# Low parts of weights made by an accumulating DMA in every fourth group of a two-layer decoder trunk

## The chip, the cores and the metric

The kernel runs on one core of one Trainium2 chip. The metric is the time of one execution in device microseconds; of several runs the median is taken. A core has five engines that matter here: TensorE (PE in the profile, its weight loads PEld), VectorE (DVE), ScalarE (ACT), GpSimd (POOL) and SyncE (SP). Each takes its instructions in order and waits on semaphores of the others.

## The reference

Two layers work on x of 256 rows and 2048 columns, all in float32. Cut to its products, a layer is:

```python
h = rmsnorm(x, norm_mix_g[i]);  proj = h @ w_in[i]      # 2048 x 9224
y_conv = conformer_conv(glu_in, ...)                    # depthwise conv, width 31, layernorm, silu, @ w_conv_out
y_attn = forgetting_attention(q, k, v, log_f) @ w_attn_out[i]      # 8 heads of 128
x = x + (sigmoid(g_conv) * y_conv + sigmoid(g_attn) * y_attn) @ w_out[i]
gate, up = split(rmsnorm(x, norm_ffn_g[i]) @ w_gate_up[i])         # 2048 x 11264
x = x + (silu(gate) * up) @ w_down[i]                              # 5632 x 2048
x = x + sigmoid(rmsnorm(x, norm_ple_g[i]) @ w_ple_gate[i]) * (p[i] @ w_ple_proj[i])
```

and a last rmsnorm follows. All weights together are some 540 MB, and each is used once.

## The kernel before, in words

Every large product runs through `chunk`: 512 columns of the output for all 256 rows, in two PSUM banks (`mm`), over groups of four blocks of 128 rows of the weight. A group is one `load`: one DMA on SP's queue brings 128 x 2048 float32 (1 MB) into a `raw` buffer, of which there are three. Then the group is split into two tiles of 1024 columns, and each tile into two parts of type float32r: the high part `wh` is the weight rounded to float32r by ScalarE (L147), and the low part `wl` is the raw weight less the high part, by VectorE (L148). The activations are split in the same manner. For each block of the weight and each half of the rows, three matmuls follow (L168 to L170): high by high, high by low part of the weight, low by high. A tile has twelve such matmuls, a group twenty-four. Of `wh` and of `wl` there are four buffers each, so a tile is prepared while up to three others are consumed, and a `raw` buffer is free for the next load when both of its tiles are converted.

There are 512 groups: 144 for `w_in` (`wI`), 16 each for `w_attn_out` and `w_conv_out` (`wA`, `wC`), 32 for `w_out`, 176 for `w_gate_up` (`wGU`), 88 for `w_down` (`wD`), 32 for `w_ple_gate` (`wPG`), and 8 of half the width for `w_ple_proj` (`wPP`). The very first group is loaded in pieces (`hook`).

Beside the products run the depthwise convolution (L336, VectorE), the attention (L495 to L532), the norms and the transposes that turn results into operands. `conv_norm` scales the convolution's result (L590 to L594) and splits it (L186, L187). Where these stand among the weights' conversions is decided by a scheduler, which orders each engine's instructions when the program is built; on each engine they then run in that order. POOL has little to do: memsets and the reciprocal square roots of the norms (L239, `rt`, and L260, `small`).

Of the kernel before, what the change touches and what calls it, by code (L numbers as in the profile page):

```python
# [12 lines left out]
AF = mybir.ActivationFunctionType  # L13
ALU = mybir.AluOpType
# [29 lines left out]
def trunk(ctx, tc, xT, xR, pT, wI, wF, wC, wA, wOut, wGU, wD, wPG, wPP, vec, bF, gF, out):  # L44
    nc = tc.nc
# [11 lines left out]
    act, dve, pe = nc.scalar, nc.vector, nc.tensor  # L57
# [70 lines left out]
    nc.gpsimd.memset(lf, 0.0)  # L128


    def load(src, n=2048, hook=None):
        raw = raws.tile([P, 2048], F32, tag="raw", name=f"raw{next(uid)}")
        if hook is None:
            nc.sync.dma_start(raw[:, :n], src)
        else:
            nc.sync.dma_start(raw[:, :512], src[:, :512])
            nc.sync.dma_start(raw[:, 512:1024], src[:, 512:1024])
            hook()
            nc.sync.dma_start(raw[:, 1024:], src[:, 1024:])
        parts = []  # L140
        step = 1024 if hook is None else 512
        for lo in range(0, n, 1024):
            h = whs.tile([P, 1024], F32R, tag="wh", name=f"wh{next(uid)}")
            l = wls.tile([P, 1024], F32R, tag="wl", name=f"wl{next(uid)}")
            for o in range(0, 1024, step):
                e = o + step
                act.activation(h[:, o:e], raw[:, lo + o : lo + e], AF.Copy)  # L147
                dve.tensor_tensor(l[:, o:e], raw[:, lo + o : lo + e], h[:, o:e].bitcast(F32), op=ALU.subtract)  # L148
            parts.append((h, l))
        return parts  # L150
# [3 lines left out]
    def chunk(groups, xs, acc, hook=None):  # L154
        n = sum(len(ks) for _, ks in groups)
        done = 0
        for src, ks in groups:
            parts = load(src, 512 * len(ks), hook)
            hook = None
            while not all(k in xs for k in ks):  # L160
                assert turns or tasks
                run()
            for j, k in enumerate(ks):
                h, l = parts[j // 2]
                cs = slice((j % 2) * 512, (j % 2 + 1) * 512)
                for b in range(2):
                    xh, xl = xs[k][:, b * P : (b + 1) * P], xs[k][:, S + b * P : S + (b + 1) * P]
                    pe.matmul(acc[b], lhsT=xh, rhs=h[:, cs], start=(done == 0), stop=False)  # L168
                    pe.matmul(acc[b], lhsT=xh, rhs=l[:, cs], start=False, stop=False)  # L169
                    pe.matmul(acc[b], lhsT=xl, rhs=h[:, cs], start=False, stop=(done == n - 1))  # L170
                done += 1
            run()
            fill(CONV)
        return acc
# [117 lines left out]
    def hook():  # L292
        load_x(0, 2, 4)
        take(0)
# [17 lines left out]
    for i in range(L):  # L312
# [392 lines left out]
        def embed(n):  # L705
            return chunk([(wPP[i, n], range(2))], ps, [bank_ms() for _ in range(2)])
# [6 lines left out]
        for n in range(N4):  # L713
            e = embed(n)
# [85 lines left out]
```

## Time and profile before

| | |
|---|---|
| median of 3 runs | 2903.79 us (2902.66 to 2904.2) |
| the profiled execution | 2902.9 us |
| its span in the profile | 2900.8 us |
| TensorE's granted clock | 0.998 |
| read from HBM | 538.91 MB, 187 GB/s over the span |

The profile is one execution seen by the hardware profiler, with times in us from the start of the span. A row of a timeline gives the start, the duration, the engine, the line of the kernel, the operation, what it writes and reads, how many instructions are merged in the row, and in brackets for how long the engine had been idle and what ended the idle time. A row of a group gives total busy time and the mean in ns of one, then the idle time ahead of the group. A row of waits gives who waited for whom, the total in us, how often, and the longest. Matmuls overlap, so the spacing of their starts tells more than their durations.

### The profile page before, as it was taken

What the parts mean: (1) busy time and instruction counts of PE and PEld (TensorE: products, weight loads), DVE (VectorE), ACT (ScalarE), POOL (GpSimd) and SP (SyncE); (2) the same over time, 40 slices, a digit from 0 to 9 for tenths busy, and PEclk for the clock granted to TensorE, in tenths of its full rate; (3) what the DMA queues carried; (4) which work ended last, traced back from release to release, by engine and by line L of the source; (5) the groups of instructions that cost most, each with busy time, mean ns of one, the idle gap of its engine ahead of it and who ended that gap; (6) DMA issues with size and microseconds to landing.
All of it is one profiled execution on the core that took longest, in us unless ns stands there. A gap on an engine that the chain in (4) does not pass through costs nothing.

```text
span 2900.8 us, 32675 instructions
## 1 busy us (share of the span) xinstructions
PE 2876.6 (99%) x13004; PEld 2381.2 (82%) x13004; DVE 1751.8 (60%) x2264; ACT 1356.2 (47%) x1642; POOL 9.5 (0%) x40
## 2 busy tenths in 40 slices
PE   8999999999999999999999999999999999999998
PEld 6888888888888888888888888888888888888886
DVE  5997745555555555555569966465555555455554
ACT  5445744444444434445554456444443444344444
POOL 0000000000000000000000000000000000000000
PEclk9999999999999999999999999999999999999999
DMA  7554455555555555555555544555555555555553
GB/s 271 174 186 163 170 193 189 189 185 188 193 188 189 192 193 193 189 188 183 186 181 181 183 166 174 190 188 189 188 189 188 190 191 189 198 190 188 189 195 139
DMA packets 77048, 543.11 MB, mean 187 GB/s; under 512 B 8800, under 2 KB 9056, under 8 KB 12256
## 3 DMA queue, kind: packets, MB, share of 16 engines
q1 hardware_dynamic: 76896, 541.04, 53.2%
q8 instruction: 101, 1.65, 0.2%
q14 instruction: 51, 0.42, 0.0%
HBM read 538.91 MB, written 2.10 MB: 187 GB/s over the span
## 4 chain that ended last, share of the span: by engine, by line
PE 94%; DVE 4%; DMA 1%; ACT 0%; issue 0%; SPq 0%; POOL 0%; ACTq 0%; POOLq 0%; DVEq 0%
PE mm L170 30%; PE mm L168 30%; PE mm L169 30%; PE ms L199 2%; DVE pair L336 2%; DVE wl L148 2%; DMA xt<-in_xR_dram 1%; PE ms L495 0%; PE ms L170 0%; PE ms L169 0%; PE ms L168 0%; PE ms L531 0%; DMA pair<-in_xT_dram 0%; ACT tmp L221 0%; PE ms L497 0%
## 5 line engine op out<-in xcount | busy, mean ns | idle before, releaser
L148 DVE TENSOR_TENSOR wl<-raw,wh 128x1024 fp32r<-128x1024 f32 (+1 forms) x1018 | 1242.0, 1222 | 1073.9 <-ACT wh L147 1072.7
L147 ACT ACTIVATE wh<-raw 128x1024 fp32r<-128x1024 f32 (+1 forms) x1018 | 1076.6, 1058 | 1414.9 <-PE mm L170 1356.7
L168 PE MATMUL mm<-wh,pair 128*128 128x512 f32 x4032 | 1579.6, 392 | 9.3 <-ACT wh L147 9.3
L170 PE MATMUL mm<-wh,pair 128*128 128x512 f32 x4032 | 1571.8, 390 | 0.0
L169 PE MATMUL mm<-wl,pair 128*128 128x512 f32 x4032 | 1571.1, 390 | 0.5 <-DVE wl L148 0.5
L168 PEld LDWEIGHTS mm<-wh,pair 128*128 128x128 f32 x4032 | 758.0, 188 | 164.4 <-ACT wh L147 10.5
L170 PEld LDWEIGHTS mm<-wh,pair 128*128 128x128 f32 x4032 | 757.7, 188 | 158.5
L169 PEld LDWEIGHTS mm<-wl,pair 128*128 128x128 f32 x4032 | 758.1, 188 | 156.7 <-DVE wl L148 1.8
L336 DVE SCALAR_TENSOR_TENSOR pair<-pair,vecs,pair 128x256 f32<-128x256 f32 x480 | 201.1, 474 | 0.0
L187 DVE TENSOR_TENSOR pair<-ms,pair 128x512 fp32r<-128x512 f32 (+1 forms) x76 | 45.1, 626 | 1.4 <-ACT pair L186 1.3
L189 ACT ACTIVATE pair<-ms,vecs 128x256 fp32r<-128x256 f32 x80 | 33.9, 466 | 16.4 <-DVE pair L190 16.4
L666 DVE TENSOR_TENSOR xt<-xt,mm 128x512 f32<-128x512 f32 x64 | 40.9, 680 | 0.0
L682 ACT ACTIVATE tmp<-mm,rt 128x512 f32<-128x512 f32 x44 | 30.0, 690 | 21.7 <-PE mm L170 21.7
L186 ACT ACTIVATE pair<-ms 128x512 fp32r<-128x512 f32 (+1 forms) x76 | 37.9, 540 | 0.6 <-PE ms L532 0.6
L683 DVE SCALAR_TENSOR_TENSOR tmp<-mm,rt,tmp 128x512 f32<-128x512 f32 x44 | 31.4, 751 | 9.9 <-ACT tmp L682 9.9
L221 ACT ACTIVATE tmp<-xt 128x512 f32<-128x512 f32 x56 | 34.6, 618 | 5.0 <-DVE xt L721 4.2
L190 DVE SCALAR_TENSOR_TENSOR pair<-ms,vecs,pair 128x256 fp32r<-128x256 f32 x80 | 35.2, 479 | 2.6 <-ACT pair L189 1.4
L199 PEld LDWEIGHTS ms<-ident,tmp 128*128 128x128 f32 x272 | 31.7, 141 | 4.5
L199 PE MATMUL ms<-ident,tmp 128*128 128x128 f32 x272 | 35.2, 272 | 0.0
L686 DVE SCALAR_TENSOR_TENSOR tmp<-mm,rt,tmp 128x512 f32<-128x512 f32 x44 | 30.9, 743 | 0.0
L510 ACT ACTIVATE tmp<-tmp,small 128x128 f32<-128x128 f32 (+1 forms) x32 | 14.5, 454 | 19.5 <-DVE small L509 19.3
L622 ACT ACTIVATE pair<-mm,rt 128x512 f32<-128x512 f32 x28 | 18.5, 684 | 5.9 <-PE mm L170 5.9
(146 smaller groups left out, 571.0 us busy)
## 6 DMA issues: line engine op xcount, KB each, us to landing
raw<-in_wGU_dram SPq DMA_DIRECT2D x176, 1024.0 KB, 4.7
raw<-in_wI_dram SPq DMA_DIRECT2D x143, 1024.0 KB, 4.7
raw<-in_wD_dram SPq DMA_DIRECT2D x88, 1024.0 KB, 4.7
raw<-in_wOut_dram SPq DMA_DIRECT2D x32, 1024.0 KB, 4.7
raw<-in_wPG_dram SPq DMA_DIRECT2D x32, 1024.0 KB, 4.7
raw<-in_wA_dram SPq DMA_DIRECT2D x16, 1024.0 KB, 4.7
raw<-in_wC_dram SPq DMA_DIRECT2D x16, 1024.0 KB, 4.7
raw<-in_wPP_dram SPq DMA_DIRECT2D x8, 512.0 KB, 3.2
```

The source lines that it names most:

```text
L147: act.activation(h[:, o:e], raw[:, lo + o : lo + e], AF.Copy)
L148: dve.tensor_tensor(l[:, o:e], raw[:, lo + o : lo + e], h[:, o:e].bitcast(F32), op=ALU.subtract)
L168: pe.matmul(acc[b], lhsT=xh, rhs=h[:, cs], start=(done == 0), stop=False)
L169: pe.matmul(acc[b], lhsT=xh, rhs=l[:, cs], start=False, stop=False)
L170: pe.matmul(acc[b], lhsT=xl, rhs=h[:, cs], start=False, stop=(done == n - 1))
L186: act.activation(hi, src, AF.Copy)
L187: dve.tensor_tensor(lo, src, hi.bitcast(F32), op=ALU.subtract)
L190: dve.scalar_tensor_tensor(lo, src, scale, hi.bitcast(F32), op0=ALU.mult, op1=ALU.subtract)
L199: pe.transpose(pt[:, kk * S + b * P : kk * S + (b + 1) * P], src(b)[:, c : c + P], ident)
L221: act.activation(tmp(), xt[:, b, n * 512 : (n + 1) * 512], AF.Square, accum_out=self.ss[:, b * 4 + n : b * 4 + n + 1],)
L336: dve.scalar_tensor_tensor(cv[c], u[c][:, j : j + S], w, cv[c], op0=ALU.mult, op1=ALU.add,)
L666: dve.tensor_tensor(xc, xc, acc[b], op=ALU.add)
```

## The change

`load` now counts its calls. In every fourth call (not the first group, and not those of half width) the low parts are made in another way: ScalarE writes the rounded weight a second time with a scale of -1 into `wl`, and a DMA issued by POOL adds the raw weight onto it. In every other of these groups the DMA takes the weight from the `raw` buffer, in the rest from DRAM once more. VectorE has no part in these groups' conversion.

```diff
+    loads = [0]
+
     def load(src, n=2048, hook=None):
+        loads[0] += 1
+        by_dma = hook is None and n == 2048 and loads[0] % 4 == 0
         raw = raws.tile([P, 2048], F32, tag="raw", name=f"raw{next(uid)}")
...
                 act.activation(h[:, o:e], raw[:, lo + o : lo + e], AF.Copy)
+                if by_dma:
+                    act.activation(l[:, o:e], raw[:, lo + o : lo + e], AF.Copy, scale=-1.0)
+                    given = src if loads[0] % 8 == 0 else raw
+                    nc.gpsimd.dma_start(l[:, o:e], given[:, lo + o : lo + e], accum_op=ALU.add)
+                    continue
                 dve.tensor_tensor(l[:, o:e], raw[:, lo + o : lo + e], h[:, o:e].bitcast(F32), op=ALU.subtract)
```

The lines behind it move: L147 of before is L151 of the changed kernel, L148 is L157, L168 to L170 are L177 to L179, and later lines stand nine further on. The negated conversion is L153, the DMA L155.

The scheduler orders the instructions anew. The rows below are from the built programs, in order on one engine, with the numbers of the buffers, which differ between the two.

POOL at the start of the program, before: the memsets for the convolution's input and the first reciprocal square roots.

```order
L128 MEMSET lf 128x256
L349 MEMSET pair_518 128x30 x3
L349 MEMSET pair_531 128x30 x3
L239 TENSOR_TENSOR rt_293<-small_290,mhalf 128x2
L349 MEMSET pair_900 128x30 x2
L260 TENSOR_TENSOR small_2694<-small_2689,mhalf 128x2
```

POOL at the same place in the changed kernel:

```order
L128 MEMSET lf 128x256
L358 MEMSET pair_522 128x30 x3
L358 MEMSET pair_535 128x30 x3
L248 TENSOR_TENSOR rt_293<-small_290,mhalf 128x2
L155 DMA wl_298<-raw_295 128x1024
L155 DMA wl_303<-raw_295 128x1024
L155 DMA wl_442<-in_wI_dram 128x1024
L155 DMA wl_447<-in_wI_dram 128x1024
L358 MEMSET pair_908 128x30 x2
```

The DMAs of the fourth and the eighth group now stand in POOL's queue, behind the first `rt`; before, POOL had nothing between `rt` and the next memset.

ScalarE where the end of the first layer's attention meets `conv_norm`, before. `wh_2930` and `wh_2934` are the two tiles of one group; L186 and L592 belong to `conv_norm`, L523 to the attention.

```order
L186 ACTIVATE pair_2863<-ms_2860 128x256
L147 ACTIVATE wh_2930<-raw_2928 128x1024
L147 ACTIVATE wh_2934<-raw_2928 128x1024
L186 ACTIVATE pair_2823<-pair_521 128x256
L186 ACTIVATE pair_2878<-pair_892 128x256
L147 ACTIVATE wh_2989<-raw_2987 128x1024
L523 ACTIVATE tmp_2919<-ms_2915 128x384
L592 ACTIVATE tmp_2922<-pair_892,vecs 128x256
```

ScalarE at the same place in the changed kernel, where this group is one of the fourth ones (`wh_2956`, `wl_2957`, and `wh_2961`, `wl_2962`):

```order
L195 ACTIVATE pair_2889<-ms_2886 128x256
L151 ACTIVATE wh_2956<-raw_2954 128x1024
L153 ACTIVATE wl_2957<-raw_2954 128x1024
L195 ACTIVATE pair_2849<-pair_525 128x256
L195 ACTIVATE pair_2904<-pair_900 128x256
L151 ACTIVATE wh_2961<-raw_2954 128x1024
L532 ACTIVATE tmp_2945<-ms_2941 128x384
L601 ACTIVATE tmp_2948<-pair_900,vecs 128x256
L153 ACTIVATE wl_2962<-raw_2954 128x1024
```

The second tile's negated conversion has moved behind two conversions of `conv_norm`, the attention's copy and a sigmoid.

TensorE at this place, before:

```order
L521 MATMUL ms_2915<-ident,tmp_2804 128x128
L168 MATMUL mm_2754<-wh_2930,pair_260 128x512
L169 MATMUL mm_2754<-wl_2931,pair_260 128x512
L170 MATMUL mm_2754<-wh_2930,pair_260 128x512
L168 MATMUL mm_2755<-wh_2930,pair_260 128x512
L169 MATMUL mm_2755<-wl_2931,pair_260 128x512
```

TensorE in the changed kernel (L530 is the L521 of before, L540 and L541 are L531 and L532):

```order
L530 MATMUL ms_2941<-ident,tmp_2830 128x128
L177 MATMUL mm_2780<-wh_2956,pair_260 128x512
L177 MATMUL mm_2781<-wh_2956,pair_260 128x512
L540 MATMUL ms_2990<-tmp_2945,pair_1287 128x256
L541 MATMUL ms_2990<-tmp_2945,pair_1287 128x128
L178 MATMUL mm_2780<-wl_2957,pair_260 128x512
L179 MATMUL mm_2780<-wh_2956,pair_260 128x512
```

The first matmul with a low part has moved back by three places, and two matmuls of the attention have moved ahead of it. The second layer has the same rows at its like place.

## The prediction

> **What bounds the kernel now.** I read the shares of busy time first, then the chain that ended last, both on the page.
>
> ```profile
> PE 2876.6 (99%) x13004; PEld 2381.2 (82%) x13004; DVE 1751.8 (60%) x2264; ACT 1356.2 (47%) x1642; POOL 9.5 (0%) x40
> ...
> PE 94%; DVE 4%; DMA 1%; ACT 0%; issue 0%; SPq 0%; POOL 0%; ACTq 0%; POOLq 0%; DVEq 0%
> ```
>
> TensorE works or streams in 99% of the span and carries 94% of the chain. The 4% of VectorE invite the thought that less work there is a gain, so next I asked for what TensorE waited. The columns are total us, times, longest:
>
> ```profile
> PE mm L168 <- ACT wh L147: 9.3, 3, 7.4
> PE ms L265 <- ACT tmp L264: 0.6, 2, 0.3
> PE mm L169 <- DVE wl L148: 0.5, 1, 0.5
> ```
>
> In the whole execution TensorE waited 0.5 us for a low part. The chain passes through VectorE where that engine is the last of several to arrive, but hardly anything is lost there. So the edit can win next to nothing, and the question is what it delays.
>
> Third, how far ahead the weights are prepared. This is the timeline of two stretches, one where VectorE is full and one where it is half idle:
>
> ```profile
> 1505.18 7.62 DVE L336 SCALAR_TENSOR_TENSOR pair<-pair,vecs,pair 128x256 f32<-128x256 f32 x19
> ...
> 1505.94 1.06 ACT L147 ACTIVATE wh<-raw 128x1024 fp32r<-128x1024 f32 x1 [1.49 <-PE mm L170]
> ...
> 1508.01 0.39 PE L169 MATMUL mm<-wl,pair 128*128 128x512 f32 x1
> 1508.23 0.39 PE L170 MATMUL mm<-wh,pair 128*128 128x512 f32 x1
> 1508.46 0.39 PE L168 MATMUL mm<-wh,pair 128*128 128x512 f32 x1
> ...
> 1508.66 1.06 ACT L147 ACTIVATE wh<-raw 128x1024 fp32r<-128x1024 f32 x1 [1.66 <-PE mm L170]
> ```
>
> ```profile
> 903.55 1.06 ACT L147 ACTIVATE wh<-raw 128x1024 fp32r<-128x1024 f32 x1 [1.66 <-PE mm L170]
> 906.27 1.06 ACT L147 ACTIVATE wh<-raw 128x1024 fp32r<-128x1024 f32 x1 [1.66 <-PE mm L170]
> ```
>
> ScalarE starts a tile of high parts (half a group) each 2.72 us in both stretches, and each time it had waited for the twelfth matmul of an older tile. Twelve matmuls a tile make 2.72 / 12 = 0.227 us each. Four buffers of each kind mean that a tile is made while three others are consumed: the last reader of a low part ends at 1508.01 + 0.39 = 1508.40, the tile four places on begins at 1508.46 + 3 x 2.72 = 1516.62, and its first low-part matmul stands one later, 1516.85. A low part therefore has 8.4 us from buffer free to first use.
>
> **The change part by part.** 252 DMAs on POOL's queue (126 groups of two), 124 of them from the raw tile in SBUF and 128 from DRAM; as many instructions leave VectorE and enter ScalarE. Their durations stand in two rows:
>
> ```profile
> L148 DVE TENSOR_TENSOR wl<-raw,wh 128x1024 fp32r<-128x1024 f32 (+1 forms) x1018 | 1242.0, 1222 | 1073.9 <-ACT wh L147 1072.7
> L147 ACT ACTIVATE wh<-raw 128x1024 fp32r<-128x1024 f32 (+1 forms) x1018 | 1076.6, 1058 | 1414.9 <-PE mm L170 1356.7
> ```
>
> VectorE loses 252 x 1.222 = 308 us, ScalarE gains 252 x 1.058 = 267 us and comes to 1623 of 2901 us. Neither is the bound before or after; value of both: 0. In 232 of the 252 cases the order now puts the negated conversion straight ahead of the high part's, so the DMA may start 1.06 us after the buffer is free, and the high part, 1.06 us later than before, still has over 5 us in hand.
>
> *The price of one accumulating DMA*, X, from the end of the negation to TensorE's go, is not in the trace. The nearest rows (issues with median us to landing; share of the queue; issue on SP; an instruction on POOL):
>
> ```profile
> q1 hardware_dynamic: 76896, 541.04, 53.2%
> ...
> raw<-in_wGU_dram SPq DMA_DIRECT2D x176, 1024.0 KB, 4.7
> ...
> raw<-in_wPP_dram SPq DMA_DIRECT2D x8, 512.0 KB, 3.2
> ...
> pin<-in_pT_dram SPq DMA_DIRECT2D x2, 256.0 KB, 4.3
> ```
>
> ```profile
> L134 SPq DMA_DIRECT2D raw<-in_wGU_dram x176: 327/328/328, 598.5 to 2673.1; - x176
> ```
>
> ```profile
> 29.50 0.70 POOL L239 TENSOR_TENSOR rt<-small,mhalf 128x2 f32<-128x2 f32 x1 [26.22 <-DVE small L237]
> ```
>
> 512 KB more cost 1.5 us, so 1.7 us are fixed. Low end: the destination's read is free and POOL issues like SP, 3.2 us. Middle: source and destination are read, 1024 KB, 4.7 us. A 256 KB load beside others took 4.3 where the line gives 2.45, 1.85 more; the engines are busy 53.2% of the time, so I add 1.0. POOL's smallest work takes 0.70 where SP's issue takes 0.33, so 0.4 more: X = 6.1, an estimate. High end: two passes, 2 x 3.2, behind a whole load's 3.0 us of data, 9.4. I take 6.1 because the row with the same bytes read is the nearest.
>
> [...]
>
> *The bulk, 123 groups.* Of 8.4 us the negation takes 1.06, so X may be 7.3. At 6.1 the DMA is hidden, by TensorE's work on three other tiles, with 1.2 us to spare. If that cover goes, every group loses X - 7.3.
>
> *SP's queue.* Where the raw tile is the source, its buffer is free for the next load only when the DMA lands. Before:
>
> ```profile
> 901.92 1.23 DVE L148 TENSOR_TENSOR wl<-raw,wh 128x1024 fp32r<-128x1024 f32 x1 [1.49 <-ACT wh L147]
> ```
>
> The load leaves when this ends, 903.15, and lands 4.7 later, 907.9; its tile is first converted six tiles after 898.1 (two periods of 2.72 before 903.55), at 914.4. Spare: 6.5 us. The release moves to about 903.55 - 2.72 + 1.06 + 6.1 = 908.0, 4.9 later: hidden. If that cover goes, the next load is late, and after it the high parts.
>
> *POOL's queue.* A DMA that waits there for its negation holds up the DMAs behind it and POOL's small work: 40 instructions of 9.5 us. Of these TensorE waits only for what follows from L260 (0.6 us in all, by way of L264), and the DMA ahead of that one has its negation a whole group earlier on ScalarE. Value: 0; if it slips, the wait at L265 grows by as much.
>
> *Three places with less cover.* Where a group's ScalarE work comes late, the order shows low-part matmuls pushed back. The first is the first chunk's fourth group, whose conversions stand behind the squares of x:
>
> ```profile
> 29.41 2.00 ACT L147 ACTIVATE wh<-raw 128x1024 fp32r<-128x1024 f32 x2 [0.39 <-DVE small L237]
> ```
>
> ```profile
> 30.52 0.73 PE L168 MATMUL mm<-wh,pair 128*128 128x512 f32 x2 [1.52 <-ACT wh L147]
> 31.78 0.50 PE L169 MATMUL mm<-wl,pair 128*128 128x512 f32 x1 [0.53 <-DVE wl L148]
> ```
>
> High part to 30.4, negation to 31.45, landing 31.45 + X. Before, the low part was used at 31.78. Two matmuls of the next group now run ahead, 0.45. Loss: 31.45 + X - 31.78 - 0.45 = X - 0.8 = 5.3. The other half has 11 matmuls (2.5 us) more and its negation ends 2.1 later: nothing.
>
> The other two are the same rows in both layers, where attention's end meets conv_norm. Layer 0:
>
> ```profile
> 342.63 2.00 ACT L147 ACTIVATE wh<-raw 128x1024 fp32r<-128x1024 f32 x2
> 344.53 0.71 ACT L186 ACTIVATE pair<-pair 128x256 fp32r<-128x256 f32 x2
> ...
> 346.09 0.48 ACT L523 ACTIVATE tmp<-ms 128x384 f32<-128x384 f32 x1
> 346.46 1.58 ACT L592 ACTIVATE tmp<-pair,vecs 128x256 f32<-128x256 f32 x3
> ```
>
> ```profile
> 344.89 0.48 PE L168 MATMUL mm<-wh,pair 128*128 128x512 f32 x1
> 345.20 0.48 PE L169 MATMUL mm<-wl,pair 128*128 128x512 f32 x1
> ```
>
> Before, both high parts run from 342.63 and TensorE is there 2.3 us later. Now: high part to 343.63, negation to 344.7, landing 344.7 + X = 350.8 against 345.20; moved ahead are one L168 and the two matmuls of L531 and L532 (0.57 together). Loss 5.0. The second half: two conversions of L186 to 345.4, high part to 346.4, L523 to 346.9, L592 to 347.4, negation to 348.4, landing 354.5; TensorE arrives 14 matmuls after 350.8, at 354.0: 0.4 more. Each layer X - 0.7 = 5.4.
>
> Sum: (X - 0.8) + 2 (X - 0.7) = 3X - 2.2 = 16.1 us. The profiled execution took 2902.9 us (span 2900.8), 0.9 below the median of 2903.79. 2902.9 + 16.1 = 2919.0. With X from 3.2 to 7.3 the sum is 7.4 to 19.7, so 2910 to 2923.
>
> **The rivals.** *The bulk is not hidden.* The point is X = 7.3. For it: only 1.2 us are spare, no row shows POOL issuing a DMA, and the second half of a group waits in the same queue behind the first. Against: engines only 53.2% busy; 252 x 3.0 us more makes 79%. Price 126 us for each us of X: at 9.4, 123 x 2.1 + 26 = 284, so 3187; at 8.3, 123 + 23, so 3049. Above 5.4 us of engine time for each DMA (46.8% of 2901 / 252) the engines themselves become the bound.
>
> *No change within 0.2%* (5.8 us, about what a measurement of this kernel can tell from none). 3X - 2.2 is below 5.8 only under X = 2.7, less than a plain load's 3.2; or the three places are covered by something that I misread. At X = 2 it gives 2907.
>
> *Faster*, by one mechanism: VectorE no longer paces TensorE in the stretch where it is full.
>
> ```profile
> 85.00:140.00 55.00, 54.88 (x252) 43.67 (x251) 55.00 (x123) 25.80 (x33) 0.00 (x0) 1.00 0.54 185
> ```
>
> It is busy for 55.00 of 55 us, yet TensorE lost 0.12 there. There are 4032 x 3 / 12 = 1008 tiles, so the 2.72 us of each would have to shrink by over 0.016 to make up for 16 us, and by 0.03 to give 2889; but it is 2.72 with VectorE full and with it half idle.
>
> *The DMA of the change does something else*, for example lands in two steps: that is a larger X, and counted there.
>
> **How the numbers follow.** Forecast (hidden but for three places) 0.57; bulk not hidden 0.32, of which 0.2 below 9.1 us; no change 0.08; faster 0.03. Hence faster 0.03, same 0.08, slower 0.89. The point is the likeliest, 2919, its own range 2910 to 2923. For 8 in 10 I leave out the two fast cases below 2908 and X above 9.1 us (123 x 1.8 + 25 = 246, so 3150): 2908 to 3150.
>
> **What would show it.** Right: the waits of TensorE name the DMA three times, each 3 to 6 us, near 31, 345 and the like place of the second layer, and in the FFN ScalarE's conversions still come each 2.72 us. X is read there as landing minus the end of the negation. Wrong: TensorE waiting for L178's operand some 120 times or more (X was too small), or an unchanged cadence with no wait at the three places (the order misled me), or ScalarE instead of the DMA as what is waited for.

## The result, and the profile after

The changed kernel takes 3067.59 us (median of 4 runs, 3065.42 to 3071.15); the kernel before, run beside it, 2903.85 us (2902.66 to 2904.2). The ratio is 1.0567, with a 95% interval of 1.0553 to 1.0581: slower by 164 us, where 2919 was predicted. The profiled execution took 3069.53 us, its span is 3067.6 us, and the granted clock was 0.983 instead of 0.998.

The shares of busy time, the DMA queues, the chain and the DMA issues on the page of the changed kernel:

```profile
PE 2933.8 (96%) x13004; PEld 2401.8 (78%) x13004; DVE 1458.4 (48%) x2012; ACT 1593.0 (52%) x1894; POOL 225.7 (7%) x292
...
q1 hardware_dynamic: 76896, 541.04, 49.0%
q0 software_dynamic: 36288, 132.14, 22.9%
...
PE 39%; DMA 9%; ACT 2%; issue 1%; DVE 1%; POOL 0%; ACTq 0%; POOLq 0%
...
raw<-in_wGU_dram SPq DMA_DIRECT2D x176, 1024.0 KB, 4.8
...
wl<-raw POOLq DMA_DIRECT2D x124, 512.0 KB, 5.8
...
wl<-in_wGU_dram POOLq DMA_DIRECT2D x44, 512.0 KB, 7.7
```

VectorE is relieved by 293 us, and nothing is won by it. DMAs have 9% of the chain, where it was 1%; the profile follows the chain back over only half of the span (its shares add up to 52%), so this says that they are in it, not how much they cost. From issue to landing, the DMAs that read the raw tile take 5.8 us, those that read `w_gate_up` in DRAM 7.7 (medians over the first and the second DMA of a group). The waits of TensorE (total us, times, longest) say which of them hurt:

```profile
PE mm L178 <- DMA wl<-in_wI_dram: 35.5, 18, 2.8
PE mm L178 <- DMA wl<-in_wGU_dram: 34.5, 23, 2.9
PE mm L178 <- DMA wl<-in_wD_dram: 17.5, 10, 3.3
...
PE mm L178 <- DMA wl<-raw: 1.9, 1, 1.9
```

Of the raw-fed DMAs one is waited for, of the DRAM-fed ones some sixty. One such place is in the timeline of ScalarE, POOL, SP and TensorE (start, duration, engine, instruction, idle time before it):

```profile
685.94 1.06 ACT L153 ACTIVATE wl<-raw 128x1024 fp32r<-128x1024 f32 x1 [1.43 <-PE mm L178]
...
688.66 1.06 ACT L153 ACTIVATE wl<-raw 128x1024 fp32r<-128x1024 f32 x1 [0.71 <-PE mm L178]
689.62 1.04 ACT L151 ACTIVATE wh<-raw 128x1024 fp32r<-128x1024 f32 x1
```

```profile
687.29 0.85 POOL L155 DMA_DIRECT2D wl<-in_wGU_dram  x1 [18.18 <-ACT wl L153]
690.01 0.86 POOL L155 DMA_DIRECT2D wl<-in_wGU_dram  x1 [1.87 <-ACT wl L153]
...
717.06 0.86 POOL L155 DMA_DIRECT2D wl<-raw  x1 [1.87 <-ACT wl L153]
```

```profile
690.69 0.33 SPq L138 DMA_DIRECT2D raw<-in_wGU_dram  x1
...
722.86 0.33 SPq L138 DMA_DIRECT2D raw<-in_wGU_dram  x1
```

```profile
699.92 0.79 PE L178 MATMUL mm<-wl,pair 128*128 128x512 f32 x1 [2.69 <-DMA wl<-in_wGU_dram]
700.51 0.63 PE L179 MATMUL mm<-wh,pair 128*128 128x512 f32 x1
700.94 0.63 PE L177 MATMUL mm<-wh,pair 128*128 128x512 f32 x1
...
702.65 0.52 PE L178 MATMUL mm<-wl,pair 128*128 128x512 f32 x1
703.00 0.39 PE L179 MATMUL mm<-wh,pair 128*128 128x512 f32 x1
```

The first two rows of POOL are a DRAM-fed group, the third is the second DMA of the next, raw-fed one. In the DRAM-fed group the raw tile is free as soon as ScalarE has converted its second half, at 690.66, and SP's next load leaves at 690.69, 0.7 us after the second DMA. That DMA lands at 699.88, the load at 700.04, 9.35 us after its issue. In the raw-fed group the raw tile stays taken until the DMA has landed, at 722.72, and the load leaves at 722.86. Over all groups, X (end of the negation to landing, medians) is 6.05 and 6.04 us for the first DMA of a DRAM-fed group and the second of a raw-fed one, 6.3 for the first of a raw-fed one, and 9.1 for the second of a DRAM-fed one; 7.3 were to be had.

What the transfers do to the engines stands in the stretches of time (us, busy time of PE, PEld, DVE, ACT, POOL with counts, granted clock, share of the DMA engines, GB/s): the two groups just shown, and then the place around the wait.

```profile
687.30:700.10 12.80, 10.11 (x45) 8.06 (x44) 3.67 (x3) 5.83 (x6) 1.70 (x2) 0.98 0.98 284
711.00:723.00 12.00, 12.00 (x55) 9.91 (x54) 3.85 (x5) 6.75 (x8) 1.71 (x2) 1.00 0.70 176
```

```profile
697.00:700.00 3.00, 0.31 (x3) 0.08 (x1) 1.22 (x1) 1.06 (x1) 0.00 (x0) 0.91 0.98 324
700.00:702.70 2.70, 2.70 (x7) 2.12 (x8) 0.00 (x0) 0.00 (x0) 0.00 (x0) 0.50 0.44 164
702.70:705.50 2.80, 2.80 (x13) 2.33 (x12) 1.67 (x3) 1.06 (x1) 0.00 (x0) 0.96 0.03 12
```

In the DRAM-fed group the DMA engines are 98% busy, in the raw-fed one 70%. And behind the wait TensorE runs at half its clock: seven matmuls in 2.7 us where thirteen follow in the next 2.8.

The starts of TensorE's matmuls give the size of both losses. I take the time from the start of each weight matmul to the start of TensorE's next instruction, less the usual 0.227 us. Where this time is over 0.6 us (waits), the excess adds up to 119.9 us, 5.1 before; where it is 0.3 to 0.6 us (half clock), to 57.0 us, 13.7 before. Together that is 158 of the 164 us: 115 of waiting and 43 of half clock.

### The profile page after: what moved, and what is told of

Same layout as the page of the kernel before. It is cut to its first block, busy times and chain, and to the rows that moved or that the text cites. A ratio compares the mean times of both kernels' runs of the same rounds, so it can differ in the third digit from the quotient of the medians.

```text
span 3067.6 us, 33507 instructions
## 1 busy us (share of the span) xinstructions
PE 2933.8 (96%) x13004; PEld 2401.8 (78%) x13004; DVE 1458.4 (48%) x2012; ACT 1593.0 (52%) x1894; POOL 225.7 (7%) x292
## 3 DMA queue, kind: packets, MB, share of 16 engines
q1 hardware_dynamic: 76896, 541.04, 49.0%
q0 software_dynamic: 36288, 132.14, 22.9%
## 4 chain that ended last, share of the span: by engine, by line
PE 39%; DMA 9%; ACT 2%; issue 1%; DVE 1%; POOL 0%; ACTq 0%; POOLq 0%
PE mm L178 13%; PE mm L179 12%; PE mm L177 12%; DMA wl<-in_wGU_dram 3%; DMA wl<-in_wI_dram 2%; DMA wl<-in_wD_dram 1%; DMA wl<-in_wPG_dram 1%; ACT wl L153 1%; PE ms L208 1%; DMA wl<-in_wOut_dram 1%; DMA wl<-in_wC_dram 0%; ACT wh L151 0%; DVE wl L157 0%; PE ms L504 0%; DVE pair L345 0%
## 5 line engine op out<-in xcount | busy, mean ns | idle before, releaser
L178 PE MATMUL mm<-wl,pair 128*128 128x512 f32 x4032 | 1595.2, 396 | 104.4 <-DMA wl<-in_wI_dram 35.5
L151 ACT ACTIVATE wh<-raw 128x1024 fp32r<-128x1024 f32 (+1 forms) x1018 | 1072.3, 1054 | 1068.5 <-PE mm L179 994.3
L177 PE MATMUL mm<-wh,pair 128*128 128x512 f32 x4032 | 1592.4, 395 | 12.5 <-ACT wh L151 12.3
L157 DVE TENSOR_TENSOR wl<-raw,wh 128x1024 fp32r<-128x1024 f32 (+1 forms) x766 | 934.7, 1221 | 1374.7 <-ACT wh L151 1374.0
L179 PE MATMUL mm<-wh,pair 128*128 128x512 f32 x4032 | 1587.0, 394 | 0.2 <-DVE pair L199 0.2
L178 PEld LDWEIGHTS mm<-wl,pair 128*128 128x128 f32 x4032 | 766.4, 190 | 289.9 <-DMA wl<-in_wGU_dram 44.8
L177 PEld LDWEIGHTS mm<-wh,pair 128*128 128x128 f32 x4032 | 766.7, 190 | 173.1 <-ACT wh L151 13.9
L179 PEld LDWEIGHTS mm<-wh,pair 128*128 128x128 f32 x4032 | 766.6, 190 | 159.7 <-DVE pair L199 0.7
L153 ACT ACTIVATE wl<-raw 128x1024 fp32r<-128x1024 f32 x252 | 267.0, 1060 | 217.7 <-PE mm L178 216.2
L155 POOL DMA_DIRECT2D wl<-raw x124 | 106.2, 856 | 1372.8 <-ACT wl L153 1268.8
L155 POOL DMA_DIRECT2D wl<-in_wGU_dram x44 | 37.7, 857 | 450.5 <-ACT wl L153 450.5
L155 POOL DMA_DIRECT2D wl<-in_wI_dram x40 | 34.3, 858 | 434.5 <-ACT wl L153 386.1
```

What stands on the lines that cost most here:

```text
L153: act.activation(l[:, o:e], raw[:, lo + o : lo + e], AF.Copy, scale=-1.0)
L155: nc.gpsimd.dma_start(l[:, o:e], given[:, lo + o : lo + e], accum_op=ALU.add)
```

## The experiments

The table has them by time, with X of the second DMA of a group, how long after that DMA's issue the next load leaves in a DRAM-fed group (a raw-fed one in brackets), and the two sums just described. All but the times are of one profiled execution each, medians or sums.

| | us | X of second DMA, DRAM / raw | next load after | waits | half clock |
|---|---|---|---|---|---|
| before | 2903.9 | | | 5.1 | 13.7 |
| changed kernel | 3067.6 | 9.1 / 6.0 | 0.7 | 119.9 | 57.0 |
| all from raw | 2920.8 | - / 6.0 | (5.8) | 15.6 | 16.1 |
| second tile alone from DRAM | 2922.9 | 6.2 / 6.1 | 3.2 | 16.6 | 18.4 |
| load held | 2929.5 | 6.2 / 6.1 | 6.7 | 17.8 | 21.0 |
| plain copy | 2959.9 | 5.3 / 3.8 | 0.7 | 45.8 | 25.8 |
| half the bytes | 2956.7 | 7.0 / 6.1 | 0.7 | 44.0 | 24.6 |
| half the bytes, half by VectorE | 2952.0 | 6.0 / 6.0 | 1.4 | 34.0 | 24.2 |
| low parts last | 2953.7 | 8.9 / 6.0 | 0.7 | 39.3 | 24.8 |
| filler | 3069.0 | 9.0 / 6.0 | 0.7 | 30.6 | 28.5 |
| five buffers | 3089.0 | 12.0 / 10.2 | 2.7 | 143.4 | 59.1 |
| five buffers, load held | 2964.9 | 9.6 / 10.2 | 9.8 | 47.0 | 28.5 |
| all from DRAM | 3215.6 | 9.4 / - | 0.7 | 237.4 | 87.0 |
| all from raw, three out | 2907.0 | - / 6.0 | (5.8) | 7.4 | 15.1 |

**What makes the DRAM-fed groups late.** Three theories stood: A, SP's next load, let go early, meets the second DMA; B, an accumulating DMA that reads DRAM is slower in itself; C, the second DMA stands behind the first in POOL's queue.

*All from raw.*

```diff
-                    given = src if loads[0] % 8 == 0 else raw
+                    given = raw
```

> All 126 groups add the raw tile from SBUF, none the weight from DRAM. X is the time from the end of the negated conversion to the DMA's landing; in the changed kernel it was 6.0 to 6.3 us, but 9.1 for the second DMA of a group fed from DRAM, and a tile can spare 7.3. Theory A (collision): a DRAM-fed group gives its raw buffer back early, SP's next 1 MB load then runs beside the group's second DMA and slows it. Theory B (source): a DRAM-fed accumulation is slow in itself. Theory C (queue): a second DMA close behind a first on POOL's queue is slow. A and B expect X of 6.0 to 6.3 throughout, waits only at the three places with less cover (about 5 + 2 x 4 us of waiting and some 5 us at a lower clock behind them): 2915 to 2928 us, granted clock 0.995 or more. C expects 126 late second DMAs and over 3150 us.

2920.84 us (2919.2 to 2922.45), ratio to before 1.0061 (1.0044 to 1.0078). The waits of TensorE and the DMA issues:

```profile
PE mm L177 <- ACT wh L151: 13.3, 3, 7.4
PE mm L178 <- DMA wl<-raw: 7.3, 5, 1.9
PE ms L540 <- ACT tmp L532: 2.0, 2, 1.0
```

```profile
wl<-raw POOLq DMA_DIRECT2D x252, 512.0 KB, 5.7
```

With the same number of accumulating DMAs, the same 132.14 MB on their queue and the same work of POOL and ScalarE, all but 18 us of the loss is gone. The second DMA of each group, behind the first in the same queue as before, has X = 6.0: C falls.

*The load held.* A POOL instruction that reads the raw tile and the landed low part keeps the raw tile taken; nothing else is moved.

```diff
                     nc.gpsimd.dma_start(l[:, o:e], given[:, lo + o : lo + e], accum_op=ALU.add)
+                    if given is src and lo:
+                        nc.gpsimd.tensor_tensor(small(2), raw[:, lo : lo + 2], l[:, 0:2].bitcast(F32), op=ALU.add)
```

> The changed kernel with its DRAM-fed groups, but behind each such group's second DMA a tiny addition on POOL reads the raw tile and the landed low part, so the raw buffer, and with it SP's next load, is held until that DMA has landed. Sources and bytes are the same. A expects X of the second DMA back at 6.0 to 6.5 and a time within 0.4% of the kernel fed from SBUF alone (2915 to 2932). B expects X = 9.1 still and 3060 us or more.

*Only the second tile from DRAM.* Here the first DMA, from raw, keeps the raw tile until it lands, so the load leaves 3.2 us after the second DMA's issue.

```diff
-                    given = src if loads[0] % 8 == 0 else raw
+                    given = src if loads[0] % 8 == 0 and lo else raw
```

> In every eighth group only the second tile is fed from DRAM, the first from the raw tile. [...] A expects X of the second DMA 6.0 to 7.2 and 2915 to 2940 us; B expects 9 us for these 64 and about 3060.

2929.54 us (1.0092, interval 1.0077 to 1.0107) and 2922.93 us (1.0068, 1.0048 to 1.0088). The DMA issues of the first of the two:

```profile
wl<-raw POOLq DMA_DIRECT2D x124, 512.0 KB, 5.9
...
wl<-in_wGU_dram POOLq DMA_DIRECT2D x44, 512.0 KB, 6.1
```

DRAM as the source costs 0.1 us by X, or nothing: B falls, and A stands. Most of the 147 us that separate the changed kernel from all-from-raw go when the load leaves 2.5 to 6 us later, though with the load held the same data is read from the same place.

**What the meeting is: bytes or a fixed delay.** Theory D: in such a group the DMA engines are full, and what is late is late by the work ahead of it. From the page, one accumulating DMA takes 22.9% x 3067.6 / 252 = 2.8 us of all 16 engines, one load (541.04 MB are 516 of them) 49.0% x 3067.6 / 516 = 2.9. Two DMAs and two loads are 11.4 us of engine time in the 12.8 us quoted above, and the load after these leaves at 696.67, within them; two DMAs and one load, in the raw-fed group, are 8.5 of 12.

*Half the bytes, half by VectorE.*

```diff
+                    if given is src and lo:
+                        nc.gpsimd.dma_start(l[:, 0:512], given[:, lo : lo + 512], accum_op=ALU.add)
+                        dve.tensor_tensor(l[:, 512:e], raw[:, lo + 512 : lo + e], h[:, 512:e].bitcast(F32), op=ALU.subtract)
+                        continue
```

> The changed kernel, but in the groups fed from DRAM the second tile's DMA carries only the first 512 of 1024 columns (those that TensorE reads first); VectorE makes the low part of the rest. Theory D (the 16 DMA engines are full in such a group, so what is late is late by the work ahead of it): a DMA takes 22.9% of 3067.6 us / 252 = 2.8 us of all engines, half of it 1.4, so X of the second DMA falls from 9.1 to about 7.7 and the time to 2935 to 2975 us. Rival (a fixed delay when a POOL-issued DMA meets a load, whatever it carries): X stays at 8.7 to 9.3, 3040 to 3070 us.

2952.0 us, as D expects, but X came to 6.0 and not to 7.7: a miss on the size. The edit also shortens the negation and lets VectorE hold the raw tile, so the load leaves 1.4 us after the DMA instead of 0.7. It can't tell bytes from that, hence one more:

```diff
-                    nc.gpsimd.dma_start(l[:, o:e], given[:, lo + o : lo + e], accum_op=ALU.add)
+                    c = 512 if given is src and lo else e
+                    nc.gpsimd.dma_start(l[:, o:c], given[:, lo + o : lo + c], accum_op=ALU.add)
```

> In the groups fed from DRAM the second DMA carries 512 of 1024 columns as in the run before it, but nothing takes its place: the negated high part of the other half stays as it is, so VectorE, the negation and the moment at which SP's next load leaves (0.7 us after the second DMA's issue) are those of the changed kernel. Theory D (engine time): 1.4 us less of it, so X of the second DMA falls from 9.1 to 6.5 to 7.8 us and the next load's 8.45 us fall too, 2925 to 2975 us. Rival (a fixed delay when the two meet): X 8.7 to 9.3 and 3040 to 3070 us; then the 6.0 us of the run before came from the load's later start alone (1.4 instead of 0.7).

Nothing is added to the other 512 columns. 2956.67 us. The load leaves after 0.7 us, X is 7.0, and that load takes 6.8 us instead of 8.45. Its DMA issues:

```profile
wl<-in_wGU_dram POOLq DMA_DIRECT2D x22, 512.0 KB, 5.9
...
wl<-in_wGU_dram POOLq DMA_DIRECT2D x22, 256.0 KB, 6.7
```

Half the bytes take 2.1 us off X and 1.6 off the load, with nothing else moved: a fixed delay is out, and D holds, though its 1.4 us were too few.

*Plain copy.* The DMA only copies the weight into the low part (no adding; the low part is then the whole weight).

```diff
-                    nc.gpsimd.dma_start(l[:, o:e], given[:, lo + o : lo + e], accum_op=ALU.add)
+                    nc.gpsimd.dma_start(l[:, o:e], given[:, lo + o : lo + e])
```

> The DMAs of the changed kernel without the addition: each copies the weight over the negated high part (the low part is then the weight itself), same sources, bytes written and queue. [...] If a DMA costs by the bytes it reads, X falls from 6.0 by about 1.5 us (512 KB by the loads' rows) to 4.3 to 4.7; if the addition is free, X stays at 6.0. For the DRAM-fed second DMA A expects it slower than the first all the same, by 0.5 to 2 us, but under the 7.3 that a tile can spare: 2908 to 2935 us.

2959.88 us in one run, above what was expected. The queue and POOL's instruction:

```profile
q0 software_dynamic: 36288, 132.14, 13.6%
```

```profile
L155 POOL DMA_DIRECT2D wl<-raw x124: 527/527/712, 31.3 to 2876.6; - x124
```

A copy takes 13.6% x 2958 / 252 = 1.6 us of the engines, the adding one 2.8; on POOL it is 0.53 us instead of 0.86. X falls by 1.2 to 3.8 us, by the place (medians). Yet 24 of the 64 second DMAs of DRAM-fed groups still have an X over 7.0 us, a tenth even 9.25 and more, and they make the waits. The trace says which. In 25 groups the load before left only 4.2 us ahead of the second DMA and is still under way at its issue (it lands 0.5 us later, median); 23 of the 24 are among them. In 26 groups that load left 5.1 us ahead and has mostly landed; there X is 5.0. In the changed kernel the two kinds of group have 9.8 and 8.4. So the second DMA meets the end of one load as well as the load behind it, and a cheaper transfer helped mainly where the first of them had landed.

Both kernels have the same 132.14 MB on this queue, so the bytes counted there do not explain 2.8 against 1.6 us. Whether the adding DMA's 1.2 us more go to reading its destination or to the adding itself, no run here separates.

*All from DRAM.*

```diff
-                    given = src if loads[0] % 8 == 0 else raw
+                    given = src
```

> All 126 groups fed from DRAM. Theory D, each such group costs the same: from the kernel with none (2920.8 us) to the changed kernel with 64 (3067.6) it is 2.29 us a group, so 126 groups give 3209 us (3190 to 3230), X of the second DMA 9.1. Rival (the backlog is carried from one such group into the next): X above 10 us and over 3250 us. Rival (it saturates because late matmuls make room): under 3170 us.

3215.62 us (1.1072, 1.1034 to 1.1109): the same 2.3 us for each DRAM-fed group, no backlog from one into the next.

**More time for the DMA.** *Low parts last*: in the DRAM-fed groups the four matmuls on `wl` come behind the eight others of their tile.

```diff
-                    pe.matmul(acc[b], lhsT=xh, rhs=l[:, cs], start=False, stop=False)
+                    if not late:
+                        pe.matmul(acc[b], lhsT=xh, rhs=l[:, cs], start=False, stop=False)
...
+                if late and j % 2:
+                    for jj in (j - 1, j):
...
```

> The changed kernel with the four matmuls that read a low part put behind the eight others of the tile, in the groups fed from DRAM alone: seven matmuls, 1.6 us, more until the first use. Theory A: the 64 second DMAs at 9.1 us are late by about 0.2 us instead of 1.8, so 2935 to 2975 us, with the clock's loss mostly gone. Rival (throughput of the DMA engines): over 3030 us.

2953.66 us (1.0171, 1.0152 to 1.019). X is still 8.9; with 1.6 us more until the first use, 81 of the 115 us of waiting and 32 of the 43 of half clock are gone.

*Five buffers for low parts* (`pool("wls", 5)` instead of 4):

> The changed kernel with five buffers for low parts instead of four, so a tile's low part has 2.72 us more from buffer free to first use: 10.0 us for X instead of 7.3. Theory A (the second DMA of the groups fed from DRAM collides with SP's next load and lands after 9.1 us, 1.8 us too late): the collision is still there (X of the second DMA 8.5 to 10 us) but mostly hidden, 2905 to 2930 us. Rival (the DMA engines cannot move the data in time, so more lead only shifts the wait): over 3000 us.

3089.01 us: slower than the changed kernel, in the rival's range, and my expectation failed. The rows of issues and waits:

```profile
wl<-raw POOLq DMA_DIRECT2D x124, 512.0 KB, 9.0
...
wl<-in_wGU_dram POOLq DMA_DIRECT2D x44, 512.0 KB, 9.7
```

```profile
PE mm L178 <- DMA wl<-in_wGU_dram: 33.4, 23, 2.1
...
PE mm L178 <- DMA wl<-raw: 18.9, 33, 1.9
```

The buffer that is free sooner lets ScalarE negate sooner, and the second half's no longer waits for TensorE: the two DMAs of a group now leave 1.54 us apart instead of 2.72, and in raw-fed groups the second leaves only 1.6 us after the load before it (4.4 in the changed kernel). All of them share the engines (92% busy from 1536 to 1551 us, where both DMAs of a DRAM-fed group leave), X grows to 8.6 to 12.0, and the 2.72 us won are spent. Raw-fed DMAs, which read nothing from DRAM, are hit too (6.0 to 10.2 for the second), so the meeting doesn't need DRAM as the source. To see whether the buffer itself cost anything, it was run with the load held as above:

> Five buffers for low parts, and in the groups fed from DRAM a small POOL instruction behind the second DMA holds the raw tile, so that SP's next load leaves only when that DMA has landed. Theory D: the two DMAs of a group are still issued 1.5 us apart and share the engines, so X stays near 9 and 10 us, but the second one of the groups fed from DRAM comes down from 12.0 to about 10.2, as in the groups fed from raw; the lead is 10.0: 2925 to 2975 us. Rival (the fifth buffer itself costs the time, by the new order on ScalarE): above 3030 us.

2964.91 us (1.0208, 1.0179 to 1.0238), X 9.6 and 10.2: as D expects. Two thirds of what five buffers lost against before go with the meeting; 35 us over four buffers with the load held (2929.5) remain, with the two DMAs of a group still 1.5 us apart.

**The half clock.** *Filler*: eight matmuls against zeros ahead of the second tile of each DRAM-fed group.

```diff
+                if loads[0] % 8 == 0 and j == 2:
+                    for b in range(8):
+                        pe.matmul(acc[b % 2], lhsT=zero, rhs=h[:, cs], start=False, stop=False)
```

> The changed kernel with eight more matmuls (128x512, against an operand of zeros, 1.8 us in all) ahead of the second tile of each of the 64 groups fed from DRAM, so that TensorE works where it now waits. They are 116 us of added work. Theory A1 (the half clock after a late low part follows from TensorE standing still): the waits are filled, starts spaced 0.43 us go from 57 us of excess to about 20, and the time is 3030 to 3062 us, less than the changed kernel's 3067.6 in spite of the added work. Rival A2 (the half clock has another cause, such as the two transfers at once): the excess stays, 3075 to 3110 us.

3068.97 us, between the two ranges, so the time decides nothing. The parts do: 512 x 0.227 = 116 us of work came in, 89 us of waits and 28.5 us of half clock went, with X at 9.0 as ever. The half clock follows TensorE's standing still, not the transfers. I had expected the filler to end nearly all waits; 25 us above before's remain.

**What is left without the meeting.**

```diff
+        by_dma = hook is None and n == 2048 and loads[0] % 4 == 0 and loads[0] not in (4, 56, 312)
```

with all from raw.

> As the kernel with all DMAs from the raw tile (2920.84 us), but the three groups at the three places with less cover (the 4th, 56th and 312th) are left to VectorE, so 123 groups go by DMA. Theory A (the loss of that kernel is the three places and nothing else): 2903 to 2908 us, within 0.2% of before, TensorE waits for a DMA's low part for under 3 us in all, granted clock 0.998. Rival (ScalarE's longer work or POOL's DMAs cost something all along): it stays at 2914 to 2921 us.

2906.98 us against 2904.11: ratio 1.0013, 1.0004 to 1.0022. By the ratios, 1.0061 and 1.0013, the three places were 0.0048, or 13.9 us. No version beats before, where waits and half clock hold 19 us in all.

## Why the prediction was wrong

*The step that failed* is "SP's queue". The prediction worked out what happens "where the raw tile is the source": the load leaves later, which is hidden. For the other half of the groups, where DRAM is the source, the raw tile is let go when only ScalarE's conversions have read it, and the load leaves beside the group's second DMA. That was not costed, and X was taken as one number for all 252 DMAs. The estimate of 6.1 holds for three kinds of four (6.0 to 6.3) and not for the second DMA of a DRAM-fed group, 9.1.

The load itself hardly moved. In the first layer's FFN it leaves 2.35 us after the start of the group's second high part where VectorE makes the low parts, before and in the changed kernel; 1.07 us in DRAM-fed and 6.34 in raw-fed groups (medians). As the negation delays that high part by 0.7 us, the load leaves 0.5 us earlier than by VectorE in the DRAM-fed groups and 4.7 later in the raw-fed ones. So the new DMA was put beside a load that had always stood there, and the raw-fed groups go free because they push it away. How much the 0.5 us add was not tested alone.

*The argument that hid it* is "engines only 53.2% busy; 252 x 3.0 us more makes 79%". The share came out at 72%, but a mean over the span says nothing of the 12.8 us in which two loads and two DMAs ask for 11.4 us of engine time and the engines are 98% busy. The numbers were there: a load was known to be 3.0 us of data and a DMA was put at as much.

*The rival "the bulk is not hidden"* had the right point, X = 7.3, and its price fits: each late group loses X - 7.3, so 64 x (9.1 - 7.3) = 115 us, and from all from raw to the changed kernel the waiting grows by 104 us. Its reason, that the second half waits in the same queue behind the first, was wrong, since in raw-fed groups it does so too and lands in 6.0. Its sign, some 120 waits for L178's operand, came out at some sixty, as half of the groups are late.

*Not in any sum*: the half clock after a wait, 41 us between the same two kernels, 0.6 us for each late group.

*Right*: that nothing is won by relieving VectorE or lost by loading ScalarE (293 us less and 237 more); X of an accumulating DMA where no load is let go beside it; and 3X - 2.2 = 16.1 us for the three places, 2919.0 in all, which is near what all from raw gives (2920.8). That the totals agree so well is in part luck. In all from raw the waits at the start are 5.4 us, 5.3 forecast, but 3.1 instead of 5.4 at each of the two ends of attention, where no load runs beside the DMA and X is 4.7; half clock, which no sum had, and places that the prediction did not name make up for it. And TensorE names the DMA for only 1.8 to 1.9 us at each place, not 3 to 6: ahead of that it is idle for 3.1 us at the start, for the next group's high part, and for 1.0 at each of the two ends, for the attention's copy (L532), as the new order has put their matmuls in front.

What X hangs on shows in the changed kernel: a raw-fed DMA has a median X of 4.9 us where no load is under way beside it (31 of them) and of 6.3 beside one (93), the second DMA of a DRAM-fed group has 9.1.

## What to carry to other kernels

Ask of every transfer that an edit adds what already runs at that time, and of every buffer whether its new release moves the next transfer into its way or out of it: here it was the load that nobody had touched. Add up the transfer engines' work over the few microseconds in which it falls due, not over the span. More buffers are not more slack if the work ahead of a transfer moves forward with them: a fifth buffer's 2.72 us were spent here, at 3089.0 us against 3067.6.

## What the hardware showed that was not expected

After a wait TensorE ran at a granted clock of 0.50 for 3.41 us, four times of 20 for twice that. Of 31 waits of 1.9 us and more in the changed kernel (by the starts of all of TensorE's matmuls, beyond the first 37 us), 20 were followed by it, at some 1.5 to 2.9 us each, 36 us together; of 38 shorter ones none but two that stand just ahead of one of the 20. In this trace it hangs on where a wait falls: all stretches of half clock start on one grid of 3.413 us. The stretches of time below are three steps of this grid, and then three around a wait of 2.64 us that was not followed by half clock:

```profile
696.07:699.49 3.42, 1.16 (x6) 0.62 (x4) 1.79 (x2) 1.06 (x1) 0.00 (x0) 1.00 1.01 319
699.49:702.90 3.41, 2.98 (x7) 2.40 (x8) 0.00 (x0) 0.00 (x0) 0.00 (x0) 0.50 0.49 183
702.90:706.31 3.41, 3.41 (x16) 2.80 (x16) 2.48 (x3) 1.06 (x1) 0.00 (x0) 1.00 0.02 7
2641.67:2645.09 3.42, 2.40 (x11) 1.66 (x9) 1.30 (x2) 1.61 (x2) 0.00 (x0) 1.00 1.04 314
2645.09:2648.50 3.41, 1.79 (x8) 1.49 (x9) 1.15 (x1) 0.00 (x0) 0.00 (x0) 1.00 0.89 329
2648.50:2651.91 3.41, 3.41 (x17) 2.83 (x16) 2.59 (x3) 1.06 (x1) 0.00 (x0) 1.00 0.06 24
```

In the first step TensorE stands still for 2.26 us (by the profile's ends of matmuls, which are modelled), and the next one runs at half clock; the second wait is cut in two by the grid, 1.02 and 1.62 us, and nothing follows. Over the changed kernel, each step at full clock with 1.77 us or more of standing still (20 of them) was followed by half clock, and none with 1.73 or less; in the kernel all from DRAM the two bounds are 1.87 and 1.83. So in these two traces a step did not have to be idle throughout: some 1.8 of its 3.41 us were enough.

A load and an accumulating DMA that met landed together, at 700.04 and 699.88, and both paid: 9.35 us for a load, of which the median is 4.7 in the kernel before, and X = 10.2, where raw-fed groups have 6.0.
